# Normalising attention: the reciprocal sums broadcast through DRAM and multiplied on GpSimd, instead of spread by TensorE and multiplied on VectorE

## The chip, the cores and the metric

The kernel runs on one core of one Trainium2 chip. The metric is the device time of one execution in microseconds (us). Three runs of the kernel before gave a median of 2939.29 us, between 2937.05 and 2940.01.

## The reference

Two layers of a diffusion backbone over 1024 latent tokens and 256 context tokens, model width 1024. Layer 0 mixes tokens with a convolution module, layer 1 with grouped-query attention (16 query heads, 4 key/value heads, head size 64, one softmax over all 1280 tokens). A SwiGLU feed-forward network follows each. The change touches only the division by the softmax sums in layer 1 and the start of the product with `wo`:

```python
def gqa_sdpa(q, k, v):
    qg = q.reshape(B, Q, N_KV_HEADS, KV_GROUP, Dh)
    s = jnp.einsum("bqkgd,bskd->bkgqs", qg, k).astype(jnp.float32) * (Dh ** -0.5)
    p = jax.nn.softmax(s, axis=-1).astype(v.dtype)
    o = jnp.einsum("bkgqs,bskd->bqkgd", p, v)
    return o.reshape(B, Q, H * Dh)
...
def attention_module(hx, hc, wq, wk, wv, wo, q_g, k_g, cos, sin, need_ctx):
    ...
    ob = lax.map(lambda q: gqa_sdpa(q, k_all, v_all), qb)
    yx = ob.transpose(1, 0, 2, 3).reshape(B, S, N_HEADS * HEAD_DIM) @ wo
...
def swiglu(h, w1, w3, w2):
    return (jax.nn.silu(h @ w1) * (h @ w3)) @ w2
```

## The kernel before, in words

Every matmul takes a high and a low part of its operands and sums the products of these parts (three in a projection: L172, L173, L174), so TensorE (PE) carries the time. Each engine works through a fixed list of instructions in order. A scheduler writes these lists beforehand from priorities: the main line of the program, background generators that are pumped between its steps (`self.bgq`, `self.pump`), and matmuls that are put back by some steps (`with self.later(self.lav)`).

Attention is cut into 32 units: one of 4 key/value heads `t` by one block of 128 queries, with the 4 query heads that share the key/value head. Two functions make a unit.

- `scores` (L1105): for each of the 4 heads the products of q and k (L1116) into PSUM, a scaling with a row minimum on VectorE (DVE, L1122), and the exponential on ScalarE (ACT, L1124), which also leaves the row sum in `sums`. The probabilities lie with queries on the partitions, 1280 keys along the row.
- `values` (L1128): in 10 steps of 128 keys, four transposes on PE (L1134) into PSUM, the high part by ACT (L1137), the low part by DVE (L1138), and two products with the values (L1140, L1141) into the PSUM bank "av". The result has head dimensions on the partitions and queries along the row, so the 4 sums of a query, which lie on that query's partition, have to get into a row and onto all partitions of their head. Before, this goes: reciprocal on DVE (L1145), a copy by GpSimd (POOL) that repeats each of the 4 numbers 64 times (L1147), two PE transposes of that copy into the bank "av" (L1155) once ACT and DVE have emptied it (L1151, L1152), and a DVE multiply with the transposed numbers (L1156). `done` then stores the tile in the DRAM tile `od` from POOL's queue (L1450); the last unit of a half stays on chip in `olast`.

`attn_stream` (L1160) drives the units: `load_q` (L1102, POOL) fetches q for the next unit, `load_k` (L1095, POOL, two halves) the keys of the next `t`. Units 0 to 15 cover the left half of the queries. The first four run beside the last projections of q, k and v, the others alone, until about 1845 us. `out_proj` then loads `od` (L1485, POOL, four loads), splits it (L161, L164), loads the residual (L1500) and multiplies by `wo`. Units 16 to 31 (right half) run as a background generator beside that product and the left half's feed-forward network, until about 2390 us; there one k buffer ("KB") serves all `t`. Their `out_proj` is followed by the right half's feed-forward network.

Tags as "T1", "T5", "HS" name large SBUF buffers. T1 and T5 hold the probabilities of three heads each during attention.

Of the kernel before, what the change touches and what calls it, by code (L numbers as in the profile page):

```python
# [8 lines left out]
F32 = mybir.dt.float32  # L9
# [3 lines left out]
ALU = mybir.AluOpType  # L13
AX = mybir.AxisListType

P = 128
# [4 lines left out]
TOK = CTX + SEQ  # L21
# [3 lines left out]
NH, NKV, HD = 16, 4, 64  # L25
# [30 lines left out]
class Kern:  # L56
# [1071 lines left out]
    def values(self, t, Ps, sums, dst, done):  # L1128
        nc, c = self.nc, self.c
        av = self.bank("av")  # L1130
        for j in range(NJ):
            tp = self.bank("pt")
            for h in range(4):
                nc.tensor.transpose(tp[:, h * P:(h + 1) * P], Ps[h][:, j * P:(j + 1) * P], c["ident"])  # L1134
            ph, pl = self.ptring[self.ptslot % len(self.ptring)]
            self.ptslot += 1
            nc.scalar.copy(ph, tp)  # L1137
            nc.vector.tensor_tensor(pl, tp, ph.bitcast(F32), op=ALU.subtract)  # L1138
            with self.later(self.lav):
                nc.tensor.matmul(av, lhsT=self.value(t, j), rhs=ph, start=j == 0, stop=False)  # L1140
                nc.tensor.matmul(av, lhsT=self.value(t, j), rhs=pl, start=False, stop=j == NJ - 1)  # L1141
            yield 0.87

        r = sums[:, 1, :]
        nc.vector.reciprocal(r, sums[:, 0, :])  # L1145
        rx = self.sb(256)
        nc.gpsimd.tensor_copy(rx.rearrange("p (h d) -> p h d", d=HD), r.unsqueeze(2).to_broadcast([P, 4, HD]))  # L1147
        tmp = self.sb(256).rearrange("p (a q) -> p a q", q=P)
        v = av.rearrange("p (a b q) -> p a b q", b=2, q=P)
        for b, r, o in ((0, slice(0, 64), slice(64, 128)), (1, slice(64, 128), slice(0, 64))):  # L1150
            nc.scalar.copy(tmp[r], v[o, :, b, :])  # L1151
            nc.vector.tensor_tensor(dst[r], v[r, :, b, :], tmp[r], op=ALU.add)  # L1152
        rb = self.bank("av")
        for a in range(2):
            nc.tensor.transpose(rb[:, a * P:(a + 1) * P], rx[:, a * P:(a + 1) * P], c["ident"])  # L1155
        nc.vector.tensor_tensor(dst, dst, rb[:, 0:256].rearrange("p (a q) -> p a q", q=P), op=ALU.mult)  # L1156
        done()
        yield 0.1

# [270 lines left out]
    def attention(self, final, qr):  # L1430
        nc, a, c = self.nc, self.a, self.c
        kbuf = self.T("T3", [P, 2 * TOK], F32R)
        pr1 = self.T("T1", [P, 3, TOK])
        prh = self.T("HS", [P, 4, TOK])
        ptt = self.T("T2", [P, 4, 2, 512], F32R)
        self.ptring = [(ptt[:, i, 0], ptt[:, i, 1]) for i in range(4)]
# [6 lines left out]
        def dst(q0):  # L1443
            def of(t, q):
                if (t, q % 4) == (NKV - 1, 3):
                    return self.olast, lambda: None
                st = self.sb(256).rearrange("p (a q) -> p a q", q=P)

                def done():
                    nc.gpsimd.dma_start(self.od[:, 2 * t:2 * t + 2, q * P:(q + 1) * P], st)  # L1450
                return st, done
            return of
# [11 lines left out]
        pr4 = None  # L1464
        for us in self.attn_stream(units, (self.kub, kbuf), dst(0), True):
            if self.bgq:
                self.pump(self.rate * us)
            elif pr4 is None:
                pr4 = self.T("T5", [P, 3, TOK])
                self.pring = self.pring[:4] + [pr4[:, 0], pr4[:, 1], pr4[:, 2]] + self.pring[4:]  # L1470
                self.set_banks(**alone)
                self.sring = [0, TOK]
# [8 lines left out]
        def out_proj(q0, otag, tags, ytag, box, xtag):  # L1481
            o = self.T(otag, [P, KT, 512])
            for q in range(4):
                n = 512 if q < 3 else 3 * P
                nc.gpsimd.dma_start(o[:, 2 * q:2 * q + 2, :n], self.od[:, 2 * q:2 * q + 2, q0:q0 + n])  # L1485
            oh = self.T(tags[0], [P, KT, 512], F32R)
            ol = self.T(tags[1], [P, KT, 512], F32R)
            for k in range(KT - 2):
# [14 lines left out]
            for k in range(KT):  # L1503
                o = self.bank("mm")
# [4 lines left out]
                w, p = (self.sm(512) for _ in range(2)) if k else more  # L1509
# [8 lines left out]
        for us in out_proj(0, "HS", ("T6", "T3"), "T4", yL, "HS"):  # L1518
            self.pump(0.4 * us)
# [6 lines left out]
        def tail_R():  # L1526
            self.set_banks(mm=[0, 1, 2, 3], st=[5, 6])
            yield from out_proj(512, "T1", ("T2", "T5"), "T1", yR, "HR")
            yield from self.post_pre2(yR, self.xv[1], self.bank("st"), self.x3d[:, :, 512:], ("T2", "T5"), fR, True)
# [21 lines left out]
        yacc, n = self.acc(CTX), CTX  # L1551
# [172 lines left out]
```

## Time and profile before

| | |
|---|---|
| median of 3 runs | 2939.29 us |
| the profiled execution | 2938.98 us, of which 2937.2 are the span |
| granted TensorE clock over the span | 0.987 |
| PE busy | 2847.7 us (97%) |
| DVE busy | 2160.7 us (74%) |
| ACT busy | 1335.5 us (45%) |
| POOL busy | 222.6 us (8%) |

The span is the time from the first to the last instruction. Busy time is the time of an engine's own instructions, without what it waits; on POOL it holds the issue of transfers where the trace gives that a duration. A share over the whole span hides stages: between 1680 and 1840 us attention runs alone, and between 1980 and 2384 us it lies beside the feed-forward network.

### The profile page before, as it was taken

The numbers are of one execution on the slowest core, as the hardware profiler recorded it, in microseconds if no ns is written. First come the engines' busy times: TensorE is split into PE (matmuls) and PEld (weight loads), VectorE is DVE, ScalarE is ACT, GpSimd is POOL, SyncE is SP. The second block draws the span as 40 slices with busy tenths as digits, with TensorE's granted clock in tenths as the row PEclk, the third lists the DMA queues.
The fourth block names the chain that finished last, engine by engine and source line by source line (L and its number), as shares of the span: only waits on it lengthen the run. The fifth ranks groups of instructions, "written<-read, shape, count | busy, mean of one in ns | idle before, by whom it ended". The sixth has DMA issues, their size and how long they took to land.

```text
span 2937.2 us, 42731 instructions
## 1 busy us (share of the span) xinstructions
PE 2847.7 (97%) x16462; PEld 2446.1 (83%) x16462; DVE 2160.7 (74%) x3746; ACT 1335.5 (45%) x2229; POOL 222.6 (8%) x377
## 2 busy tenths in 40 slices
PE   7999989999999999999999999989999999999998
PEld 6888877888888889989888787767777778889997
DVE  6887788847556378877786899786666666786777
ACT  5222255532222245544445688645555543444444
POOL 0000001011022001000011111110000000010000
PEclk9999999999999999999999999999999999999999
DMA  6443444334356224333345211322222143353332
GB/s 249 140 120 98 116 131 145 135 116 143 115 175 198 65 74 165 114 104 112 109 156 170 88 46 46 97 87 81 66 73 83 60 149 99 110 170 104 102 98 75
DMA packets 131755, 336.58 MB, mean 115 GB/s; under 512 B 31328, under 2 KB 52864, under 8 KB 130656
## 3 DMA queue, kind: packets, MB, share of 16 engines
q1 hardware_dynamic: 78016, 222.33, 24.1%
q0 software_dynamic: 29344, 103.83, 10.7%
q10 hardware_dynamic: 24192, 7.70, 1.1%
q8 instruction: 129, 2.11, 0.3%
q14 instruction: 74, 0.61, 0.1%
HBM read 289.50 MB, written 38.93 MB: 112 GB/s over the span
## 4 chain that ended last, share of the span: by engine, by line
PE 86%; DVE 7%; ACT 2%; issue 2%; DMA 2%; ACTq 0%; POOL 0%; SPq 0%; DVEq 0%; POOLq 0%
PE ps L172 15%; PE ps L173 15%; PE ps L174 15%; PE ps L875 4%; PE ps L877 4%; PE ps L876 4%; PE ps L1116 4%; PE ps L1134 4%; PE ps L1140 2%; PE ps L454 2%; PE ps L455 2%; PE ps L456 2%; PE ps L1141 2%; PE ps L185 1%; PE ps L183 1%
## 5 line engine op out<-in xcount | busy, mean ns | idle before, releaser
L172 PE MATMUL ps<-T,wh 128*128 128x512 f32 (+1 forms) x1360 | 502.5, 370 | 1.4 <-ACT T L161 0.8
L174 PE MATMUL ps<-T,wl 128*128 128x512 f32 (+1 forms) x1360 | 500.4, 368 | 2.0 <-DVE wl L148 2.0
L173 PE MATMUL ps<-T,wh 128*128 128x512 f32 (+1 forms) x1312 | 481.4, 367 | 0.2 <-DVE T L164 0.2
L144 ACT CAST wh<-wr 128x1024 fp32r<-128x1024 f32 (+1 forms) x217 | 225.0, 1037 | 419.9 <-PE ps L173 307.2
L148 DVE TENSOR_TENSOR wl<-wr,wh 128x1024 fp32r<-128x1024 f32 (+1 forms) x217 | 261.9, 1207 | 168.5 <-ACT wh L144 167.1
L875 PE MATMUL ps<-T,wh 128*128 128x256 f32 x1092 | 310.7, 285 | 5.0 <-ACT wh L161 4.5
L876 PE MATMUL ps<-T,wh 128*128 128x256 f32 x1092 | 306.5, 281 | 0.0
L877 PE MATMUL ps<-T,wl 128*128 128x256 f32 x1092 | 305.4, 281 | 0.2 <-DVE wl L164 0.2
L1138 DVE TENSOR_TENSOR T<-ps,T 128x512 fp32r<-128x512 f32 x320 | 216.8, 687 | 107.6 <-ACT T L1137 106.8
L172 PEld LDWEIGHTS ps<-T,wh 128*128 128x128 f32 x1360 | 257.8, 190 | 43.7 <-ACT T L1506 1.7
L174 PEld LDWEIGHTS ps<-T,wl 128*128 128x128 f32 x1360 | 257.7, 190 | 42.4 <-DVE wl L148 2.2
L173 PEld LDWEIGHTS ps<-T,wh 128*128 128x128 f32 x1312 | 248.5, 189 | 38.2 <-DVE T L164 1.3
L1137 ACT CAST T<-ps 128x512 fp32r<-128x512 f32 x320 | 186.0, 586 | 191.1 <-PE ps L1134 177.6
L173 PE MATMUL ps<-HS,wh 128*128 128x512 f32 x656 | 257.9, 393 | 0.0
L172 PE MATMUL ps<-HS,wh 128*128 128x512 f32 x608 | 238.4, 392 | 0.9 <-ACT wh L144 0.9
L174 PE MATMUL ps<-HS,wl 128*128 128x512 f32 x608 | 237.5, 391 | 0.0
L875 PEld LDWEIGHTS ps<-T,wh 128*128 128x128 f32 x1092 | 206.1, 189 | 11.2 <-ACT wh L161 6.7
L876 PEld LDWEIGHTS ps<-T,wh 128*128 128x128 f32 x1092 | 206.6, 189 | 0.5
L877 PEld LDWEIGHTS ps<-T,wl 128*128 128x128 f32 x1092 | 206.2, 189 | 0.6 <-DVE wl L164 0.4
L1134 PE MATMUL ps<-cst,T 128*128 128x128 f32 x1100 | 189.6, 275 | 3.2 <-DVE T L1138 3.1
L1122 DVE TENSOR_SCALAR_CACHE_REDUCE T<-ps,rq 128x1280 f32<-128x1280 f32 x110 | 170.0, 1546 | 27.9 <-PE ps L1116 22.1
L1134 PEld LDWEIGHTS ps<-cst,T 128*128 128x128 f32 x1100 | 132.6, 141 | 49.5 <-DVE T L1138 30.8
(377 smaller groups left out, 6195.9 us busy)
## 6 DMA issues: line engine op xcount, KB each, us to landing
wr<-in_w SPq DMA_DIRECT2D x170, 512.0 KB, 3.6
wr<-in_pw SPq DMA_DIRECT2D x35, 512.0 KB, 3.5
HV<-in_wmodT POOLq DMA_DIRECT2D x56, 256.0 KB, 4.1
q<-in_wmodT POOLq DMA_DIRECT2D x56, 256.0 KB, 3.9
KB<-in_w SPq DMA_DIRECT2D x24, 512.0 KB, 3.6
HR<-in_w SPq DMA_DIRECT2D x23, 512.0 KB, 3.7
q<-in_w SPq DMA_DIRECT2D x23, 512.0 KB, 4.2
q<-qsd POOLq DMA_DIRECT2D x32, 256.0 KB, 3.3
```

Of the source, the lines that this page charges most:

```text
L144: nc.scalar.copy(hi, raw)
L148: nc.vector.tensor_tensor(lo, raw, hi.bitcast(F32), op=ALU.subtract)
L172: nc.tensor.matmul(out[:, :n], lhsT=wh, rhs=xh, start=k == 0, stop=False)
L173: nc.tensor.matmul(out[:, :n], lhsT=wh, rhs=xl, start=False, stop=False)
L174: nc.tensor.matmul(out[:, :n], lhsT=wl, rhs=xh, start=False, stop=k == nk - 1)
L875: nc.tensor.matmul(out, lhsT=wh, rhs=bh, start=first and k == 0, stop=False, **skip)
L876: nc.tensor.matmul(out, lhsT=wh, rhs=bl, start=False, stop=False, **skip)
L877: nc.tensor.matmul(out, lhsT=wl, rhs=bh, start=False, stop=k == 3, **skip)
L1122: nc.vector.tensor_scalar(out=pt, in0=sc, scalar1=rq[:, h:h + 1], scalar2=None, op0=ALU.mult, op1=ALU.min, accum_out=mn)
L1134: nc.tensor.transpose(tp[:, h * P:(h + 1) * P], Ps[h][:, j * P:(j + 1) * P], c["ident"])
L1137: nc.scalar.copy(ph, tp)
L1138: nc.vector.tensor_tensor(pl, tp, ph.bitcast(F32), op=ALU.subtract)
```

## The change

`values` takes the reciprocal at its start and stores the 4 by 128 numbers in a DRAM tile `rsd[unit]` with the head outermost. Two loads bring them back, each number repeated over 64 partitions, into `rb`, at the end of the buffers T1 and T5 (one place while T5 isn't taken, then two in turn). GpSimd multiplies by `rb`. The four loads of `od` for the left half's output projection are issued by SyncE (SP), those of the right half still by POOL.

```diff
--- before.py
+++ after.py
@@ -1128,6 +1128,15 @@
     def values(self, t, Ps, sums, dst, done):
         nc, c = self.nc, self.c
         av = self.bank("av")
+        r = sums[:, 1, :]
+        nc.vector.reciprocal(r, sums[:, 0, :])
+        rd = self.rsd[self.unit]
+        rb = self.rbs[self.unit % len(self.rbs)]
+        self.unit += 1
+        nc.gpsimd.dma_start(rd.rearrange("h q -> q h"), r)
+        rv = rd.rearrange("(a b) q -> b a q", b=2)
+        for b in range(2):
+            nc.gpsimd.dma_start(rb[b * HD:(b + 1) * HD], rv[b:b + 1].to_broadcast([HD, 2, P]))
         for j in range(NJ):
             tp = self.bank("pt")
             for h in range(4):
@@ -1141,19 +1150,12 @@
                 nc.tensor.matmul(av, lhsT=self.value(t, j), rhs=pl, start=False, stop=j == NJ - 1)
             yield 0.87
 
-        r = sums[:, 1, :]
-        nc.vector.reciprocal(r, sums[:, 0, :])
-        rx = self.sb(256)
-        nc.gpsimd.tensor_copy(rx.rearrange("p (h d) -> p h d", d=HD), r.unsqueeze(2).to_broadcast([P, 4, HD]))
         tmp = self.sb(256).rearrange("p (a q) -> p a q", q=P)
         v = av.rearrange("p (a b q) -> p a b q", b=2, q=P)
         for b, r, o in ((0, slice(0, 64), slice(64, 128)), (1, slice(64, 128), slice(0, 64))):
             nc.scalar.copy(tmp[r], v[o, :, b, :])
             nc.vector.tensor_tensor(dst[r], v[r, :, b, :], tmp[r], op=ALU.add)
-        rb = self.bank("av")
-        for a in range(2):
-            nc.tensor.transpose(rb[:, a * P:(a + 1) * P], rx[:, a * P:(a + 1) * P], c["ident"])
-        nc.vector.tensor_tensor(dst, dst, rb[:, 0:256].rearrange("p (a q) -> p a q", q=P), op=ALU.mult)
+        nc.gpsimd.tensor_tensor(dst, dst, rb, op=ALU.mult)
         done()
         yield 0.1
 
@@ -1430,7 +1432,12 @@
     def attention(self, final, qr):
         nc, a, c = self.nc, self.a, self.c
         kbuf = self.T("T3", [P, 2 * TOK], F32R)
-        pr1 = self.T("T1", [P, 3, TOK])
+        def place(tag):
+            t = self.T(tag, [P, 3 * TOK + 2 * P])
+            return t[:, :3 * TOK].rearrange("p (i n) -> p i n", i=3), t[:, 3 * TOK:].rearrange("p (a q) -> p a q", q=P)
+        pr1, rb = place("T1")
+        self.rbs, self.unit = [rb], 0
+        self.rsd = self.dp.tile([2 * NKV * 4, 4, P], F32, tag="rsd", name="rsd")
         prh = self.T("HS", [P, 4, TOK])
         ptt = self.T("T2", [P, 4, 2, 512], F32R)
         self.ptring = [(ptt[:, i, 0], ptt[:, i, 1]) for i in range(4)]
@@ -1466,7 +1473,8 @@
             if self.bgq:
                 self.pump(self.rate * us)
             elif pr4 is None:
-                pr4 = self.T("T5", [P, 3, TOK])
+                pr4, rb = place("T5")
+                self.rbs.append(rb)
                 self.pring = self.pring[:4] + [pr4[:, 0], pr4[:, 1], pr4[:, 2]] + self.pring[4:]
                 self.set_banks(**alone)
                 self.sring = [0, TOK]
@@ -1482,7 +1490,8 @@
             o = self.T(otag, [P, KT, 512])
             for q in range(4):
                 n = 512 if q < 3 else 3 * P
-                nc.gpsimd.dma_start(o[:, 2 * q:2 * q + 2, :n], self.od[:, 2 * q:2 * q + 2, q0:q0 + n])
+                eng = nc.gpsimd if q0 else nc.sync
+                eng.dma_start(o[:, 2 * q:2 * q + 2, :n], self.od[:, 2 * q:2 * q + 2, q0:q0 + n])
             oh = self.T(tags[0], [P, KT, 512], F32R)
             ol = self.T(tags[1], [P, KT, 512], F32R)
             for k in range(KT - 2):
```

POOL's list before, some two units of attention alone. `qsd`, `ksd`, `od` and `rsd` are DRAM tiles, `sb` an output tile of a unit (or, before, the repeated numbers); DMASW are counts of landed transfers.

```order
L1102 DMA q_13572<-qsd_80 128x4x128 [waits DMASW4_49,PE_49]
L1450 DMA od_82<-sb_14960 128x2x128 [waits DVE_49]
L1147 COPY sb_15213<-sums_14964 128x256 [waits DMASW6_49,DVE_49,Pool_49]
L1147 COPY sb_15344<-sums_15095 128x256 [waits DMASW1_49,DVE_49,Pool_49]
L1450 DMA od_82<-sb_15093 128x2x128 [waits DMASW2_49,DVE_49]
L1102 DMA q_13572<-qsd_80 128x4x128 [waits DMASW7_49,DMASW3_49,PE_49]
```

Two copies of the repeated numbers and two loads of q stand next to each other. POOL's list after at the same place, one unit; T1 and T5 are the places of `rb`.

```order
L1136 DMA rsd_13570<-sums_14957 128x4x1 [waits DVE_49]
L1139 DMA T5_14072<-rsd_13570 64x2x128 [waits DMASW4_49,DMASW3_49]
L1139 DMA T5_14072<-rsd_13570 64x2x128 [waits DMASW5_49]
L1102 DMA q_13573<-qsd_80 128x4x128 [waits PE_49]
L1158 TENSOR_TENSOR sb_14953<-sb_14953,T1_13569 128x256 [waits DMASW7_49,DMASW0_49,DVE_49]
L1457 DMA od_82<-sb_14953 128x2x128 [waits Pool_49]
L1136 DMA rsd_13570<-sums_15087 128x4x1 [waits DVE_49]
```

Each unit now has a store to `rsd` that waits for DVE, two loads that wait for its landing, the q load behind them, the multiply of the unit before and its od store.

DVE's list before at the same place: `ps` is PSUM, T2 the split transposes, HS and T1 probabilities, `sums` the 4 sums of a query.

```order
L1152 TENSOR_TENSOR sb_14960<-ps_72,sb_15084 64x256 [waits DMASW0_49,Activation_49,Pool_49]
L1138 TENSOR_TENSOR T2_13571<-ps_72,T2_13571 128x512 [waits DVE_49]
L1122 TENSOR_SCALAR HS_13570,mn_15168<-ps_72,rq2_10629 128x1280 [waits PE_49]
L1152 TENSOR_TENSOR sb_14960<-ps_72,sb_15084 64x256 [waits Activation_49]
L1138 TENSOR_TENSOR T2_13571<-ps_72,T2_13571 128x512 [waits DVE_49,Activation_49]
L1156 TENSOR_TENSOR sb_14960<-sb_14960,ps_72 128x256 [waits DVE_49,PE_49]
L1122 TENSOR_SCALAR T1_13569,mn_15201<-ps_72,rq2_10629 128x1280
L1138 TENSOR_TENSOR T2_13571<-ps_72,T2_13571 128x512 [waits PE_49,Activation_49] x2
L1145 RECIPROCAL sums_14964<-sums_14964 128x4
L1145 RECIPROCAL sums_15095<-sums_15095 128x4 [waits Activation_49]
```

The multiply (L1156) stands in the list, and two units' reciprocals stand next to each other behind the second unit's last scaling. DVE's list after (L1147 is the low part, L1157 the add).

```order
L1122 TENSOR_SCALAR T1_13569,mn_15131<-ps_72,rq2_10629 128x1280 [waits PE_49]
L1157 TENSOR_TENSOR sb_14953<-ps_72,sb_15078 64x256 [waits DMASW5_49,Activation_49,Pool_49]
L1147 TENSOR_TENSOR T2_13572<-ps_72,T2_13572 128x512 [waits DVE_49]
L1147 TENSOR_TENSOR T2_13572<-ps_72,T2_13572 128x512 [waits Activation_49]
L1122 TENSOR_SCALAR HS_13571,mn_15164<-ps_72,rq2_10629 128x1280 [waits PE_49]
L1157 TENSOR_TENSOR sb_14953<-ps_72,sb_15078 64x256 [waits Activation_49]
L1147 TENSOR_TENSOR T2_13572<-ps_72,T2_13572 128x512 [waits Activation_49]
L1122 TENSOR_SCALAR T1_13569,mn_15197<-ps_72,rq2_10629 128x1280 [waits PE_49]
L1147 TENSOR_TENSOR T2_13572<-ps_72,T2_13572 128x512 [waits DVE_49,PE_49,Activation_49]
L1147 TENSOR_TENSOR T2_13572<-ps_72,T2_13572 128x512 [waits PE_49,Activation_49]
L1132 RECIPROCAL sums_15087<-sums_15087 128x4 [waits DMASW0_49,Activation_49]
```

The multiply is gone, and each unit has its own reciprocal (L1132) two steps behind its last scaling.

POOL's list before at the first reload of "KB" in the right half (about 2008 us).

```order
L1147 COPY sb_17026<-sums_16441 128x256 [waits DVE_49,Activation_49]
L1450 DMA od_82<-sb_16439 128x2x128 [waits DMASW3_49,DVE_49]
L1095 DMA KB_12756<-ksd_81 64x2560 [waits DMASW4_49,PE_49]
L1095 DMA KB_12756<-ksd_81 64x2560 [waits DMASW5_49]
L1450 DMA od_82<-sb_16794 128x2x128 [waits DMASW6_49,DVE_49]
L1102 DMA q_13572<-qsd_80 128x4x128 [waits DMASW7_49]
```

The two halves of the k load are issued one behind the other. POOL's list after at this place.

```order
L1158 TENSOR_TENSOR sb_16423<-sb_16423,T5_14072 128x256 [waits DVE_49]
L1457 DMA od_82<-sb_16423 128x2x128 [waits DMASW0_49,Pool_49]
L1095 DMA KB_12756<-ksd_81 64x2560 [waits DMASW1_49,PE_49]
L1158 TENSOR_TENSOR sb_16777<-sb_16777,T1_13569 128x256 [waits DMASW7_49,DMASW6_49,DVE_49]
L1095 DMA KB_12756<-ksd_81 64x2560 [waits DMASW2_49]
L1457 DMA od_82<-sb_16777 128x2x128 [waits DMASW3_49,Pool_49]
L1102 DMA q_13573<-qsd_80 128x4x128 [waits DMASW4_49]
```

The multiply of the unit before (the fourth row) now stands between the two halves of the k load.

## Rows read from the trace of the kernel before

**Rows 1.** Page, part 1: busy us, share of the span, instructions

```profile
PE 2847.7 (97%) x16462; PEld 2446.1 (83%) x16462; DVE 2160.7 (74%) x3746; ACT 1335.5 (45%) x2229; POOL 222.6 (8%) x377
```

**Rows 2.** By stretch: length, busy PE, PEld, DVE, ACT, POOL; clock, DMA share, GB/s

```profile
1680.00:1840.00 160.00, 156.12 (x940) 128.01 (x938) 145.72 (x239) 129.56 (x219) 22.38 (x37) 1.00 0.16 44
1980.00:2384.00 404.00, 403.96 (x2083) 317.76 (x2082) 265.55 (x389) 219.04 (x344) 27.98 (x45) 1.00 0.25 75
```

**Rows 3.** Chain of waits by line, 1980 to 2384 us, then 1680 to 1840

```profile
by line: PE ps L173 17.4%; PE ps L172 17.4%; PE ps L174 17.3%; PE ps L1134 15.5%; PE ps L1116 14.7%; PE ps L1140 8.3%; PE ps L1141 8.1%; PE ps L1155 1.1%; issue 0.1%
...
by line: PE ps L1134 21.3%; PE ps L1116 18.1%; PE ps L1140 15.0%; PE ps L1141 14.0%; DVE T L1138 8.7%; issue 8.2%; ACT T L1137 4.3%; DVE T L1122 4.0%; DVE HS L1122 2.3%; DVE sb L1152 2.2%; PE ps L1155 1.4%; ACT sb L1151 0.6%; ACT T L1124 0.
```

**Rows 4.** By line: count, ns min/median/max, first and last start, shape

```profile
L1155 PE MATMUL ps<-cst,sb x64: 270/273/303, 1646.9 to 2391.7; 128*128 128x128 f32 x64
...
L1147 POOL COPY sb<-sums x32: 394/402/1365, 1605.4 to 2363.0; 128x256 f32<-128x256 f32 x32
...
L1156 DVE TENSOR_TENSOR sb<-sb,ps x30: 409/410/421, 1647.3 to 2364.2; 128x256 f32<-128x256 f32 x30
```

**Rows 5.** Pieces of the chain at two units: start, us, what

```profile
1738.17 0.22 PE ps L1155 x2
...
2045.40 0.41 PE ps L1155 x2
```

**Rows 6.** PE's waits, 1680 to 1840 us: us in total, times, longest

```profile
PE ps L1116 <- DVE HS L1122: 2.8, 5, 0.6
```

**Rows 7.** Timeline: start, us, instruction, idle before and its releaser

```profile
1737.43 0.74 PE L1116 MATMUL ps<-KB,q 128*128 128x256 f32 x3 [0.56 <-DVE HS L1122]
1738.23 0.79 POOL L1102 DMA_DIRECT2D q<-qsd  x1 [9.06 <-PE ps L1116]
...
1742.03 0.18 DVE L1145 RECIPROCAL sums<-sums 128x4 f32<-128x4 f32 x1 [0.39 <-ACT T L1124]
```

**Rows 8.** Timeline, POOL: od stores four units apart

```profile
1709.77 0.71 POOL L1450 DMA_DIRECT2D od<-sb  x1 [0.20 <-issue]
...
1768.60 0.71 POOL L1450 DMA_DIRECT2D od<-sb  x1 [0.19 <-issue]
```

**Rows 9.** DMA issues: issuer, count, KB each, median us to landing

```profile
q<-qsd POOLq DMA_DIRECT2D x32, 256.0 KB, 3.3
...
KB<-ksd POOLq DMA_DIRECT2D x10, 640.0 KB, 7.1
...
od<-sb POOLq DMA_DIRECT2D x30, 128.0 KB, 2.6
...
vc<-HR ACTq DMA_DIRECT2D x7, 128.0 KB, 3.4
```

**Rows 10.** Timeline, the first reload of KB in the right half

```profile
2008.39 1.07 POOL L1095 DMA_DIRECT2D KB<-ksd  x2 [19.04 <-PE ps L1116]
...
2011.60 0.43 DVE L1152 TENSOR_TENSOR sb<-ps,sb 64x256 f32<-64x256 f32 x1 [0.21 <-ACT sb L1151]
...
2018.00 1.41 PE L1116 MATMUL ps<-KB,q 128*128 128x256 f32 x6
```

**Rows 11.** Timeline, the left half's last od store and o load

```profile
1852.66 0.43 DVE L1152 TENSOR_TENSOR sb<-ps,sb 64x256 f32<-64x256 f32 x1
...
1854.44 0.73 POOL L1450 DMA_DIRECT2D od<-sb  x1 [3.59 <-DVE sb L1156]
...
1856.99 0.72 POOL L1485 DMA_DIRECT2D HS<-od  x1 [1.83 <-DMA od<-sb]
...
1860.72 0.83 ACT L161 CAST T<-HS 128x768 fp32r<-128x768 f32 x1 [2.05 <-DMA HS<-od]
...
1862.09 0.50 PE L1140 MATMUL ps<-T,HR 128*128 128x512 f32 x1 [1.18 <-ACT T L1137]
```

**Rows 12.** Timeline, a copy of POOL beside a VectorE operation

```profile
2133.81 1.22 DVE L148 TENSOR_TENSOR wl<-wr,wh 128x1024 fp32r<-128x1024 f32 x1
...
2133.91 1.36 POOL L1147 COPY sb<-sums 128x256 f32<-128x256 f32 x1
```

## The prediction

> **What bounds the kernel now.** I read the page first: PE is busy for 97% of the span [rows 1], so a change pays mainly by what it takes off PE, and costs by what makes PE wait. An average over stages hides where PE does wait, so the busy time by stretch came next [rows 2]. The reader is to see two stages that differ. Between 1980 and 2384 us PE is busy for 403.96 of 404 us: a microsecond of PE work that goes there is a microsecond of time. Between 1680 and 1840 us, with attention alone, PE is busy for 156.1 of 160 us, and DVE stands at 145.7, ACT at 129.6. The 3.9 us without PE work are waits for the other engines, and an operation that leaves DVE could matter there. Third, the chain of waits of both stretches [rows 3]: the two transposes that go (L1155) hold 1.1% of the one and 1.4% of the other. The multiply that leaves DVE (L1156) is in neither list, though other DVE lines hold some 17% of the second (8.7, 4.0, 2.3 and 2.2). POOL is busy for 8%; it is not a matter of its load but of what stands in its list behind a wait.
>
> **What goes from PE.** 64 transposes, two a unit, each 0.27 us by its record [rows 4]. Records overlap, so the price is their share in the chain. In the long stretch that is 1.1% of 404, 4.4 us, for the 14 of the 16 right-half units that end in it: 0.32 us a unit, between the 0.22 and the 0.41 that single pieces show [rows 5]. The two units outside it (about 1921 and 2391 us) stand where PE waits now and then, and I count 0.15 us each. Term one: -4.7 us. Its bounds: -6.6 at 0.41 for all 16, -3.1 at 0.22 for 14.
>
> **Attention alone.** The chain holds 1.4% of 160, 2.2 us, of these transposes there. Yet PE waits 3.9 us in the same stretch, mostly for DVE's scaling [rows 6], and the lists change. The first score products behind a late scaling wait 0.56 us, and a wait of this kind comes in every second unit [rows 6, 7]: units run in pairs now, with two reciprocals next to each other. In the new lists every unit looks alike, each with its own reciprocal two steps behind the last scaling, where the reciprocal waits for the exponential as one of each pair does now (0.39 us [rows 7]). I take the larger wait for all: 10 units at 0.56 are 5.6 us against 3.9 now, +1.7. Against that go the 2.2 us of the transposes. Term two: -0.5 us. Bounds: -6.1 if DVE's relief (a multiply of 0.41 us a unit, [rows 4]) removes all waits as well (2.2 + 3.9), and +1.7 if waits grow to 0.78 us a unit (7.8 - 3.9 - 2.2).
>
> **Units 0 to 3 and the turn to the output projection.** The four units beside the projections lose eight transposes, 0.22 us a unit of chain by the smaller piece [rows 5], 0.9 us; PE also waits there, and I keep half: -0.5. At the turn the last od store of the left half leaves at 1854.44, waiting for DVE's multiply; its landing lets the last load of `od` go at 1856.99, ACT's split waits for that until 1860.72 in front of casts, and PE waits 1.18 us behind these [rows 11]. In the new order POOL multiplies as soon as the second add is done (1852.66 + 0.43 = 1853.09). At 0.4 to 0.6 us the store is ready about 1853.7 instead of 1854.4. SP waits for the landing instead of POOL, with nothing behind it in its list that is due before the load of a later piece of `wo`. I count that half a microsecond comes through: -0.5. Term three: -1.0 us together, bounds -2.1 (0.9 and the whole 1.18) and 0.
>
> **What POOL gets.** A unit adds a store to `rsd`, two broadcast loads and a multiply, and loses the copy of 0.40 us [rows 4]. Nothing of this is in the trace. The multiply is bounded by the copy's own rows: as many elements, but one tile read where the multiply reads two; 0.40 in the median and 1.36 at the worst, which fell beside a DVE operation that reads two tiles [rows 12]. I take 0.5 and keep 1.4. The Trainium skill, "GPSIMD Engine Reference", Engine selection, says that elementwise operations with two inputs belong on VectorE, since GpSimd is about half as fast; by its 4497 ns for 2048 columns a multiply of 256 would take 0.56 us, an estimate. By that the sum stays as it is wherever the multiply has room, and no row of this trace has such an operation on POOL to agree or not.
>
> Where it has room: the od stores of four units are 58.8 us apart (1709.77 to 1768.60 [rows 8]), 14.7 us a unit, and the new work on POOL is two or three issues of 0.7 to 0.8 us and the multiply, so its list isn't full. What counts is the order. The q load, which left at once when the scores freed its place (1738.23 [rows 7]), now stands behind a store that waits for DVE's reciprocal, and behind two loads that wait for the store's landing. Call T the end of the scores. The reciprocal starts at T + 3.8 (1742.03 - 1738.23), and takes 0.18. Then X for the store from issue to landing, 1.1 for the two issues, as for two halves of k (1.07 [rows 10]), and 3.3 for q [rows 9]. q is there at T + 8.4 + X. It is needed about one unit later, at T + 14.7; with half a microsecond to spare, at T + 14.2. So nothing is lost while X is below 5.8 us. The nearest rows: the od store of 128 KB lands in 2.6, a load in 1024 pieces of 128 bytes (`vc`) in 3.4 [rows 9]. The store to `rsd` has 512 elements that lie apart in DRAM. I take 4, which costs nothing; the bounds are 2.6 and, as the longest landing that any of these rows has, 7.1 for the k load, which would cost 1.3 us a unit.
>
> The same shift meets one k load. In the right half "KB" is reloaded three times, and at the first one the multiply of unit 18 now stands between the two halves. That unit's second add ends at 2011.60 + 0.43 = 2012.03 [rows 10]; with 0.4 to 1.4 us for the multiply the second half is issued at 2012.4 to 2013.4 instead of 2009, and lands by the k row's 7.1 us [rows 9] at 2019.5 to 2020.5. The products that need it start at 2018.00 [rows 10]; the same list is 0.4 us longer on PE up to that point, as the order has it by the durations of these rows. PE may do other work of the feed-forward network meanwhile only as far as its fixed list has it ahead. I take 0.4 us: the median landing is of two halves together, so a single half comes sooner. Bounds 0 and 1.9. Term four: +0.4.
>
> DVE loses 32 multiplies of 0.41 us, 13 us, hidden behind PE except in the stage alone, where term two has it. At the very end the split of the right half's `od` waits for POOL's last multiply instead of DVE's: within 1 us either way, counted at nothing.
>
> **Sum.** -4.7 - 0.5 - 1.0 + 0.4 = -5.8 us on the profiled execution's 2938.98, which lies 0.3 us below the median: 2933.2 us.
>
> **Rivals.** (1) *The store to `rsd` lands late* and q arrives behind its products, unit after unit in the stage alone. For it: the store stands in front of q in the list, and scattered single elements have no row here. Against it: 1024 small pieces land in 3.4 us [rows 9]. It decides from X = 5.8. At X = 8 each of 11 units waits 2.2 us, +24.2: 2957 us. The Trainium skill, "DMA: Bandwidth & Descriptors", Rules for kernel authors, speaks for this rival: a last dimension that isn't contiguous becomes one descriptor per element, and its Specifications want 512 bytes a transfer at least. By it the store is 512 descriptors of 4 bytes; how long those take no run here shows yet.
>
> (2) *DVE's relief counts fully.* If the stage alone loses its waits with the multiply, term two is -6.1: 2927.6 us. For it: DVE is at 91% there and its lines hold 17% of the chain. Against it: the multiply itself isn't in that chain.
>
> (3) *Waits eat the gain.* Stage alone +1.7, the k load late by 1.9, nothing at the turn and beside the projections: -4.7 + 1.7 + 1.9 = -1.1, 2937.9 us. For it: PE's waits come from a DVE order that gets no looser. Against it: the long stretch has no wait that could grow, but for that one load.
>
> **How the numbers follow.** Forecast 0.53, rival 1 0.15, rival 2 0.15, rival 3 0.17. What a measurement can tell from no change is 0.2%, 5.9 us, so faster means below 2933.4. The forecast stands on that line: I put 0.28 of it below and 0.25 above, so faster 0.43 with rival 2, same 0.42 with rival 3, slower 0.15. The forecast's own range is 2930 to 2936. The range for 8 in 10 reaches to rival 2 and past rival 3, and to a small part of rival 1 (X about 6.5, +8): 2927 to 2945.
>
> **What would show it.** In the profile after: PE has 64 instructions fewer, and 1980 to 2384 us gets shorter by about 4.5 us with PE still busy throughout (term one). The stage alone keeps PE waits of about half a microsecond for L1122 at each unit (term two). The last load of `od` leaves at least half a microsecond earlier against the split (term three). The store to `rsd` lands in under 5.8 us, and PE has no wait for q. I would be wrong if PE waits for a q load in the stage alone, if POOL's multiply takes over 1.5 us as a rule, or if PE's waits for DVE in that stage vanish.

## The result, and the profile after

Over 21 runs each the changed kernel takes 2944.88 us in the median (2941.54 to 2946.92) and the kernel before 2940.90 (2937.05 to 2944.93). The ratio is 1.0015, with an interval from 1.0009 to 1.0021: 4.4 us slower, between 2.6 and 6.2. The forecast was 5.8 us faster. The profiled execution of the changed kernel has a span of 2943.7 us.

The busy line of the changed kernel's page, and then its two stretches of [rows 2], with the turn to the output projection between them.

```profile
PE 2845.3 (97%) x16398; PEld 2445.9 (83%) x16398; DVE 2150.6 (73%) x3714; ACT 1336.1 (45%) x2229; POOL 293.2 (10%) x469
```

The windows (length, busy time of PE, PEld, DVE, ACT and POOL, clock, DMA share, GB/s):

```profile
1680.00:1840.00 160.00, 153.93 (x915) 125.65 (x915) 141.43 (x229) 130.94 (x217) 48.66 (x70) 1.00 0.25 54
1840.00:1890.00 50.00, 39.84 (x201) 31.08 (x200) 33.84 (x53) 31.69 (x54) 12.06 (x17) 0.90 0.41 105
1980.00:2384.00 404.00, 403.57 (x2065) 319.03 (x2064) 266.01 (x383) 222.43 (x347) 60.59 (x88) 1.00 0.37 81
```

PE has the 64 instructions fewer, and in the long stretch it is still busy for 403.6 of 404 us. The turn is another matter: of 50 us PE works 39.84, and the granted clock, which stands behind the busy times, is 0.90 in the mean. In the kernel before, the same 50 us have 47.15 and 1.00:

```profile
1840.00:1890.00 50.00, 47.15 (x247) 36.92 (x247) 39.11 (x63) 34.30 (x58) 9.12 (x13) 1.00 0.37 119
```

Where the time went is seen best by how much later the same instruction starts in the changed kernel. I took ACT's instructions in both traces, paired by line and count, and the median of nine around each mark, counted from 1590 us on (the parts of the program before that are the same, and single executions differ there by several microseconds either way):

| stretch of the kernel before | later in the changed kernel |
|---|---|
| 1590 to 1842 us, units 0 to 14 | -0.3 us |
| 1842 to 1889 us, the turn | +9.0 us |
| 1889 to 1976 us | +0.7 us |
| 1976 to 2372 us, the right half beside the feed-forward network | -3.4 us |
| 2372 to 2901 us | 0.0 us |

So one place of 50 us lost more than the other stages gained. The stretch from 1889 to 1976 us is 0 to 1.7 us longer in the runs below, 1.7 also where no store to `rsd` exists (the doubled store and the multiply on VectorE apart), and the last one is 1.8 us shorter to 1.0 longer; so nothing is read from these two rows. The timeline of the changed kernel at the turn (start, us, instruction, idle time before and what ended it):

```profile
1846.68 0.77 POOL L1136 DMA_DIRECT2D rsd<-sums  x1 [0.77 <-DVE sums L1132]
...
1848.96 1.44 SPq L1494 DMA_DIRECT2D HS<-od  x3
...
1856.56 1.20 POOL L1139 DMA_DIRECT2D T<-rsd  x2 [9.11 <-DMA rsd<-sums]
1860.32 0.62 ACT L161 CAST T<-HS 128x512 fp32r<-128x512 f32 x1 [8.26 <-DMA HS<-od]
...
1862.33 1.12 PE L1143 MATMUL ps<-cst,T 128*128 128x128 f32 x4 [8.74 <-DVE T L1147]
```

The longest piece of the chain of waits in this stretch (start, us, what):

```profile
1848.96 11.34 DMA HS<-od
```

POOL issues unit 15's store to `rsd` at 1846.68, and its landing, for which the next instruction of POOL waits 9.11 us, comes at 1856.5. In that time SP issues the first three loads of `od` (1848.96). The first of them lands 11.34 us later, ACT's split waits for it (8.26 us idle), ACT's and DVE's work for the rest of unit 15 stands behind that split in their lists, and PE waits 8.74 us. In [rows 11] it was 1.18. What the transfer engines did meanwhile stands in the busy time by stretch (columns as above), here of the changed kernel:

```profile
1850.00:1855.00 5.00, 3.59 (x24) 2.65 (x22) 2.02 (x4) 1.54 (x3) 0.00 (x0) 1.00 0.23 41
...
1863.00:1865.00 2.00, 2.00 (x9) 1.60 (x8) 1.56 (x3) 1.67 (x4) 1.30 (x2) 0.50 0.01 4
```

In the kernel before, where POOL issued the same three loads at 1848.28:

```profile
1850.00:1855.00 5.00, 4.52 (x28) 3.29 (x27) 4.57 (x9) 4.15 (x9) 1.41 (x3) 1.00 0.84 299
```

With the store in flight 41 GB/s were moved behind the issue of the loads, without it 299. The engines' recorded busy share is 0.23 in that time instead of 0.84, so the loads were held up by something that the trace doesn't show as traffic. The row from 1863 us lies behind PE's idle time: PE is busy again throughout, at a granted clock of 0.50, which is 1.2 instead of 2.4 GHz. The transfers (issuer, count, KB each, median us to landing) of the changed kernel:

```profile
od<-sb POOLq DMA_DIRECT2D x30, 128.0 KB, 4.6
...
HS<-od SPq DMA_DIRECT2D x3, 512.0 KB, 12.1
...
rsd<-sums POOLq DMA_DIRECT2D x32, 2.0 KB, 9.8
...
HS<-od SPq DMA_DIRECT2D x1, 384.0 KB, 3.4
```

The three loads in the kernel before:

```profile
HS<-od POOLq DMA_DIRECT2D x3, 512.0 KB, 5.3
```

A transfer of 2 KB takes 9.8 us, more than any of the others here but the loads beside it. The three loads of `od` beside it take 12.1 us instead of 5.3; the fourth, issued by SP too but after the store had landed, 3.4. Also od's stores take 4.6 instead of 2.6 [rows 9]. The theory from this (A): the store to `rsd` keeps the transfer engines for its 9 to 10 us, others queue behind it, and at the turn the loads of `od` are on the path. The rival (B): SP's queue is slow for these loads.

### The profile page after: what moved, and what is told of

Its sections match the earlier page's. It is cut to its first block, busy times and chain, and to the rows that moved or that the text cites. A ratio compares the mean times of both kernels' runs of the same rounds, so it can differ in the third digit from the quotient of the medians.

```text
span 2943.7 us, 42638 instructions
## 1 busy us (share of the span) xinstructions
PE 2845.3 (97%) x16398; PEld 2445.9 (83%) x16398; DVE 2150.6 (73%) x3714; ACT 1336.1 (45%) x2229; POOL 293.2 (10%) x469
## 2 busy tenths in 40 slices
DMA packets 135371, 340.84 MB, mean 116 GB/s; under 512 B 33376, under 2 KB 55152, under 8 KB 134272
## 3 DMA queue, kind: packets, MB, share of 16 engines
q0 software_dynamic: 31872, 106.13, 11.6%
## 4 chain that ended last, share of the span: by engine, by line
PE 85%; DVE 9%; ACT 3%; issue 2%; DMA 1%; ACTq 0%; SPq 0%; DVEq 0%
PE ps L172 15%; PE ps L173 15%; PE ps L174 15%; PE ps L875 4%; PE ps L877 4%; PE ps L876 4%; PE ps L1116 4%; PE ps L1143 4%; PE ps L454 2%; PE ps L456 2%; PE ps L455 2%; PE ps L1149 2%; PE ps L1150 2%; PE ps L185 1%; PE ps L183 1%
## 5 line engine op out<-in xcount | busy, mean ns | idle before, releaser
L1147 DVE TENSOR_TENSOR T<-ps,T 128x512 fp32r<-128x512 f32 x320 | 215.1, 686 | 112.5 <-ACT T L1146 111.6
```

## The experiments

Each was timed in five rounds beside the kernel before on the same chip. Times are medians, ratios are against the kernel before with the 95% interval. Most intervals reach 0.0009 of the time, 2.6 us, to either side; smaller differences between two of these kernels are not told apart.

**SP's issue undone.**

```diff
-                eng = nc.gpsimd if q0 else nc.sync
+                eng = nc.gpsimd
```

> The changed kernel with the four loads of od for the left half issued by POOL again (everything else as changed). Theory A: unit 15's store to rsd, 512 scattered elements, lands only after 9 us and delays every transfer in flight beside it, so the loads of od took 11 to 12 us. Here POOL has them behind unit 15's broadcast loads, so they are issued after that store has landed (about 1858 us instead of 1849), land in 4 to 6 us, and the split starts 1 to 3 us later than in the changed kernel: time 0 to +3 us against the changed kernel (2944.9), so 2945 to 2948. Theory B: SP's queue is slow for this tensor. Then the loads also land in 4 to 6 us here; B and A differ in what stands behind the loads in the second experiment. If the changed kernel's SP issue were the whole loss, the time would fall to about 2936.

2945.31 us, ratio 1.0022 (1.0013 to 1.0030): the loss stays. The timeline of this kernel at the turn:

```profile
1844.52 0.77 POOL L1136 DMA_DIRECT2D rsd<-sums  x1 [1.19 <-DVE sums L1132]
...
1853.43 1.20 POOL L1139 DMA_DIRECT2D T<-rsd  x2 [8.15 <-DMA rsd<-sums]
...
1854.63 2.18 POOL L1494 DMA_DIRECT2D HS<-od  x3
...
1862.85 1.12 PE L1143 MATMUL ps<-cst,T 128*128 128x128 f32 x4 [8.36 <-DVE T L1147]
```

Its transfers of `od`:

```profile
HS<-od POOLq DMA_DIRECT2D x3, 512.0 KB, 6.4
```

POOL comes to the loads only after the store has landed (8.15 us of waiting), they then take 6.4 us, and PE waits 8.36 us. The loads meet the same store either way: by SP as traffic beside them, by POOL as an instruction ahead of them.

**SP's issue alone**, in the kernel before.

```diff
-                nc.gpsimd.dma_start(o[:, 2 * q:2 * q + 2, :n], ...
+                eng = nc.gpsimd if q0 else nc.sync
+                eng.dma_start(o[:, 2 * q:2 * q + 2, :n], ...
```

> The kernel before with only one part of the change: the four loads of od for the left half issued by SP. No store to rsd exists here. Theory A (the store to rsd in flight slows the loads): they land in 4 to 6 us as in the kernel before, time 2940 to 2941.5, -0.5 to +0.5 against before. Theory B (SP's queue is slow for them): they land in 11 to 12 us, PE waits 8 to 9 us at the turn, time 2947 to 2950.

2940.92 us, ratio 1.0002 (0.9993 to 1.0011). The loads land in 4.7 us, by the transfers of this kernel:

```profile
HS<-od SPq DMA_DIRECT2D x3, 512.0 KB, 4.7
```

Theory B falls: without the store SP's loads are no slower than POOL's 5.3 us of the kernel before. They gain nothing either.

**Unit 15 without the store.**

```diff
+        onchip = self.unit == 15
...
-        nc.gpsimd.dma_start(rd.rearrange("h q -> q h"), r)
...
+        if not onchip:
+            nc.gpsimd.dma_start(rd.rearrange("h q -> q h"), r)
...
+        if onchip:
+            rx = self.sb(256)
+            nc.gpsimd.tensor_copy(rx.rearrange("p (h d) -> p h d", d=HD), r4.unsqueeze(2).to_broadcast([P, 4, HD]))
...
+        else:
+            nc.gpsimd.tensor_tensor(dst, dst, rb, op=ALU.mult)
```

> The changed kernel, but unit 15 (the last one before the output projection's first loads) takes the old way: POOL copy, two PE transposes, DVE multiply, no store to rsd and no broadcast loads. Units 0 to 14 and 16 to 31 as changed, SP issues the loads of od. Theory A: no store to rsd is in flight when the loads of od are issued, they land in 4 to 6 us instead of 11 to 12, PE's 8.7 us wait goes back to 1 to 2 us, and the half clock behind it goes too: 8 to 9.5 us less than the changed kernel, 2935.5 to 2937. Theory B (SP's queue): loads still 11 to 12 us, time 2944 to 2945.

2936.69 us, ratio 0.9992 (0.9983 to 1.0001): some 7 us less than the changed kernel by the ratios, 8 by the medians, from one store of 32. The turn in this kernel's busy time by stretch:

```profile
1840.00:1890.00 50.00, 46.66 (x242) 35.97 (x241) 36.42 (x57) 33.51 (x57) 9.36 (x14) 1.00 0.49 124
```

PE's waits there (waited for, us in total, times, longest):

```profile
PE ps L1146 <- DVE T L1150: 1.6, 1, 1.6
```

And the transfers:

```profile
HS<-od SPq DMA_DIRECT2D x3, 512.0 KB, 5.2
...
rsd<-sums POOLq DMA_DIRECT2D x31, 2.0 KB, 10.0
```

The other 31 stores still land in 10.0 us, the loads of `od` in 5.2, PE's longest wait at the turn is 1.6 us, the turn loses 1.1 us instead of 9.0 (counted as above), and the clock is 1.00 there. So the lower clock of the changed kernel (0.90 over these 50 us) came behind the idle PE and went with it.

**What in the store is slow.** First, the same 2 KB in runs of 16 bytes.

```diff
-        nc.gpsimd.dma_start(rd.rearrange("h q -> q h"), r)
+        nc.gpsimd.dma_start(rd.rearrange("h q -> (h q)").rearrange("(q h) -> q h", h=4), r)
```

> The changed kernel with the store to rsd written so that each partition's four numbers lie next to each other in DRAM: 128 runs of 16 bytes instead of 512 scattered elements of 4 bytes, the same 2 KB. The loads read the tile as before, so the numbers go to wrong queries: the output is not normalised as the reference has it, only times are read. Theory A with the scattered elements as its reason: the store lands in 2.5 to 5 us instead of 9.8 and holds up others less; the loads of od land in 4 to 7 us, time 6 to 9.5 us less than the changed kernel, 2935.5 to 2939. Theory C (any small store to DRAM whose landing is waited for lasts 9 us, or the count of elements decides): landing stays at 8 to 10 us, loads of od at 10 to 12, time 2944 to 2946.

2938.14 us, ratio 0.9996 (0.9987 to 1.0004). Transfers of this kernel:

```profile
od<-sb POOLq DMA_DIRECT2D x30, 128.0 KB, 2.3
...
HS<-od SPq DMA_DIRECT2D x3, 512.0 KB, 6.8
...
rsd<-sums POOLq DMA_DIRECT2D x32, 2.0 KB, 1.8
```

PE's waits at the turn:

```profile
PE ps L1143 <- DVE T L1147: 3.1, 1, 3.1
```

The store lands in 1.8 us, and the stores of `od` are back at 2.3. The loads of `od` take 6.8 us. Unit 15's broadcast loads now run beside them (issued at 1846.72, the loads at 1847.02), which may be why; no run separates it. PE's wait is 3.1, and the turn loses 2.7 us.

Second, 512 single elements still, but each 64 bytes from the next.

```diff
-        self.rsd = self.dp.tile([2 * NKV * 4, 4, P], F32, ...
+        self.rsd = self.dp.tile([2 * NKV * 4, 4, P, 16], F32, ...
...
-        nc.gpsimd.dma_start(rd.rearrange("h q -> q h"), r)
+        nc.gpsimd.dma_start(rd[:, :, 0].rearrange("h q -> q h"), r)
```

> The changed kernel with the 512 elements of 4 bytes each in a line of 64 bytes of its own in DRAM (the changed kernel has 16 neighbours from 16 partitions in each line). The broadcast loads read the first 2 KB of that tile, mostly zeros set once at the start of attention, so the output is not the reference's; only times are read. Theory D (the count of single elements decides): the store lands in 8 to 11 us, loads of od in 10 to 13, time 2943 to 2947. Theory E (elements that share a line wait for each other): it lands in 2 to 5 us, loads of od in 5 to 7, time 2937 to 2940.

2936.95 us, ratio 0.9985 (0.9977 to 0.9994). Transfers of this kernel:

```profile
HS<-od SPq DMA_DIRECT2D x3, 512.0 KB, 6.6
...
rsd<-sums POOLq DMA_DIRECT2D x32, 2.0 KB, 2.2
```

PE's waits at the turn:

```profile
PE ps L1143 <- DVE T L1147: 1.6, 1, 1.6
```

As many single elements land in 2.2 us, and the turn loses 0.9 us instead of 9.0 with a store still in it: it was the store's duration that cost. Neither their count nor that they are single makes the store slow by itself, and the trace counts no more packets for the slow layout (33376 of under 512 bytes in the whole changed kernel, as many with runs of 16 bytes, 33392 here). It takes single elements of different partitions that lie side by side in DRAM; the runs of 16 bytes lie side by side too, but are a quarter as many. The experiment moved all elements further apart, so it does not tell the 4 bytes between neighbours from the 512 between the heads. The Trainium skill, "DMA: Bandwidth & Descriptors", Specifications, says that a transfer below 512 bytes becomes a read, a change and a write back. That alone would make both layouts alike; here they differ by a factor of 4.5. That such writes wait for each other where they share a stretch of memory would fit, if few and longer pieces cost little, but no run showed it by itself.

**The store doubled**, its second copy to a tile that nothing reads.

```diff
         nc.gpsimd.dma_start(rd.rearrange("h q -> q h"), r)
+        nc.gpsimd.dma_start(self.rsd2[self.unit - 1].rearrange("h q -> q h"), r)
```

> The changed kernel with one suspected cost doubled: every unit stores its reciprocals a second time, to a tile that nothing reads. Theory A (the store itself keeps the transfer engines, and others queue behind it): the loads of od have two such stores ahead, land in 18 to 21 us instead of 11 to 12, and the time rises by 6 to 10 us to 2951 to 2955. Theory C (the store's landing is only a late message and holds up nobody): the loads land as in the changed kernel, time 2944 to 2946.

3086.93 us, ratio 1.0491 (1.0473 to 1.0509), from four timed runs: 147 us more than before and some 140 more than the changed kernel, where theory A expected 6 to 10. POOL's loads of `rsd` in three units of the timeline:

```profile
1743.21 1.21 POOL L1140 DMA_DIRECT2D T<-rsd  x2 [21.35 <-DMA rsd<-sums]
...
1827.74 0.61 POOL L1140 DMA_DIRECT2D T<-rsd  x1 [23.66 <-DMA rsd<-sums]
...
1904.52 0.61 POOL L1140 DMA_DIRECT2D T<-rsd  x1 [13.13 <-DMA rsd<-sums]
```

PE's waits between 1680 and 1840 us:

```profile
PE ps L1116 <- DMA q<-qsd: 18.7, 6, 8.3
```

The first and the third row are eight units apart: 161.3 us, 20.2 a unit instead of 14.7, about two stores of 10 us one behind the other. POOL waits up to 23.66 us for a landing, and PE waits for q, 18.7 us in this stretch. So two stores did not pass side by side, as they could if only a message came late; theory C falls. Theory A had the direction alone. The loads of `od` land in 9.8 us, where it expected 18 to 21. I had counted the doubled store at the turn alone, and it fills every unit: 71 us are lost before 1842, 23 at the turn and 45 in the long stretch. In the changed kernel the store of a unit takes 9.8 of its 14.7 us, which PE doesn't see; that edge was near.

**Only the right half changed.**

```diff
+        onchip = self.unit < 16
```

> Units 0 to 15 take the old way (POOL copy, two PE transposes, DVE multiply, no store to rsd), units 16 to 31 the new one; the reciprocal is early in both, and SP issues the loads of od. Theory A: the change's gain lies in the long stretch of the right half, where PE is never idle, and its loss at the turn only. The gain of the long stretch stays (-3 to -4.5 us against before), the turn is as in the kernel before: 2935 to 2936.5, a little above or at the kernel with only unit 15 on chip. Rival: the gain comes from attention alone (DVE's relief); then this run is within 1 us of before.

2940.52 us, ratio 0.9998 (0.9989 to 1.0007): 0.6 us below before, where 3 to 4.5 were expected; 3 lies at the interval's edge. In the trace the long stretch has its gain (-3.3 us between 1976 and 2372, counted as above), but 0.8 us are lost before 1842 and 0.9 at the turn: the early reciprocal alone already gives DVE another order, and PE's waits for the scaling, here between 1680 and 1840 us, grow from 3.9 to 5.9 us (3.7 and 2.2):

```profile
PE ps L1116 <- DVE HS L1122: 3.7, 6, 0.7
PE ps L1116 <- DVE T L1122: 2.2, 5, 0.6
```

**Runs of 16 bytes with the right numbers, unit 15 on chip.**

```diff
-        nc.gpsimd.dma_start(rd.rearrange("h q -> q h"), r)
...
+            nc.gpsimd.dma_start(rd.rearrange("(q h) -> q h", h=4), r)
+            rbt = self.sb(512)
+            for b in range(2):
+                nc.gpsimd.dma_start(rbt[b * HD:(b + 1) * HD, 0:511], rd[b:b + 511].unsqueeze(0).to_broadcast([HD, 511]))
+            rb = rbt.rearrange("p (q a c) -> p c a q", a=2, c=2)[:, 0]
```

> A version meant to beat both: unit 15 on chip as before, all other units store their reciprocals in runs of 16 bytes, two loads of 2044 contiguous bytes to 64 partitions each bring all four heads' numbers (into a small tile), and POOL's multiply picks every second pair with a stride. Theory A: the store lands in about 2 us, nothing is held up, the turn is as before, the gain of the long stretch comes in full: 3 to 5 us below before, 2934.5 to 2936.5, the same as or up to 1.5 us below the kernel with only unit 15 on chip. If holding up transfers costs nothing in the long stretch, it equals that kernel.

2939.23 us, ratio 0.9994 (0.9985 to 1.0002). The store lands in 1.8 us, and yet it is not faster than the kernel with scattered stores and unit 15 on chip. Away from the turn the slow stores cost nothing that these runs can tell. In the profiled execution, with a span of 2939.7 us, 4.1 us were lost before 1590 us, where nothing was changed, so it says as little.

**The left half exactly as before, the right half as changed**, with POOL's loads of `od` and the late reciprocal for units 0 to 15.

```diff
+        onchip = self.unit < 16
+        if not onchip:
+            nc.vector.reciprocal(r, sums[:, 0, :])
...
+        if onchip:
+            nc.vector.reciprocal(r4, sums[:, 0, :])
...
-                eng = nc.gpsimd if q0 else nc.sync
+                eng = nc.gpsimd
```

> The left half (units 0 to 15) exactly as in the kernel before, with the late reciprocal, the copy, transposes and DVE multiply, and POOL's loads of od; the right half (units 16 to 31) as changed. Differs from the run with the right half alone changed in that the left half's lists are those of before. Theory A: attention alone and the turn are then as before to within 0.3 us (PE's waits for the scaling between 1605 and 1845 us fall from 11.0 back to about 8.9), and only the long stretch's gain of 3.3 us is left: 2936 to 2937.5 when before is at 2940. Rival: the gain of the long stretch is given back behind it (as its end moves against the loads of the next stage); then within 1 us of before.

2937.63 us, ratio 0.9987 (0.9978 to 0.9996): faster than both kernels, by the ratio 3.8 us below the one before. Its turn in the busy time by stretch:

```profile
1840.00:1890.00 50.00, 47.69 (x249) 37.43 (x249) 38.46 (x61) 34.11 (x58) 11.09 (x16) 1.00 0.48 121
```

PE's waits in attention alone:

```profile
PE ps L1116 <- DVE HS L1122: 2.8, 5, 0.6
PE ps L1116 <- DVE T L1122: 1.0, 5, 0.2
```

And in the long stretch:

```profile
PE ps L1116 <- DMA KB<-ksd: 0.5, 1, 0.5
```

The turn and the waits of attention alone are those of the kernel before, PE waits 0.5 us once for a k load in the long stretch, and that stretch keeps its gain (-3.4 us between 1976 and 2372). Together with the run on the right half alone, which differs in the left half's reciprocal, copy and loads, this puts the 0.8 us lost before 1842 down to the left half's lists.

**The same with runs of 16 bytes in the right half.**

```diff
+            nc.gpsimd.dma_start(rd.rearrange("(q h) -> q h", h=4), r)
+            rbt = self.sb(512)
...
```

> As the run before it, but the right half stores its reciprocals in runs of 16 bytes and reads them back as one row of 2044 bytes a partition. Theory A: nothing of the right half waits for the store, so its landing in 2 instead of 10 us changes nothing on PE: the same time as the run before it to within 1.5 us. Rival: the scattered stores cost the long stretch something by holding up its weight loads; then 1 to 2 us less than the run before it.

2936.83 us, ratio 0.9989 (0.9981 to 0.9998): the same within what these runs tell, and the long stretch gains 3.2 us instead of 3.4. If the slow stores hold up weight loads there, it doesn't reach PE.

**The multiply back on VectorE.**

```diff
-        nc.gpsimd.tensor_tensor(dst, dst, rb, op=ALU.mult)
+        nc.vector.tensor_tensor(dst, dst, rb, op=ALU.mult)
```

> The changed kernel with the multiply on VectorE again (operands as changed, rb in SBUF). Theory A: the multiply's engine is off the path in every stage but attention alone, where 0.41 us a unit go back to a DVE at 88%: 0 to +2 us against the changed kernel, 2944.5 to 2947. Rival (POOL's 0.75 us multiply, slower than DVE's 0.41, delays the od stores and the turn): 1 to 3 us less than the changed kernel.

2951.50 us, ratio 1.0039 (1.0025 to 1.0053), from five timed runs: some 7 us more than the changed kernel, where I expected 0 to 2. In the trace 2.2 us are lost between 1590 and 1842, where the changed kernel gained 0.3. The rest could not be put at a place: the lists of the right half come out in another order, so that the same instruction is 4.6 us later between 1976 and 2372 and 5.5 earlier behind that, -0.9 us together where the changed kernel has -3.4. How much of it is the multiply and how much the other order stays open.

## Why the prediction was wrong

**What bounds it** was right: what PE loses in the long stretch is time.

**Term one (-4.7)** had the right mechanism, at too high a price. The chain share of 1.1% priced a unit at 0.32 us; the stretch with 14 units got 3.4 us shorter. The 0.4 us of term four's wait is in that, so the transposes gave some 3.8, 0.27 a unit, and nearer to the smaller piece of [rows 5], 0.22, than to 0.41. In every run with the right half on `rsd` and the multiply on POOL, the doubled store apart, the stretch got 2.9 to 3.7 shorter; with SP's issue alone it stayed the same (+0.1). Why the share told too much was not looked into.

**Term two (-0.5) and units 0 to 3 (-0.5)** came out at -0.3 together, for -1.0. The wait of the first scores behind a late scaling came at every unit, as the lists had it: PE's waits for DVE's scaling between 1680 and 1840 us rose to 6.6 us, from the 2.8 of [rows 6] and 1.1 for the other buffer; 5.6 were forecast. The row for the other buffer in the kernel before:

```profile
PE ps L1116 <- DVE T L1122: 1.1, 5, 0.2
```

In the changed kernel:

```profile
PE ps L1116 <- DVE HS L1122: 3.6, 6, 0.6
PE ps L1116 <- DVE T L1122: 3.0, 5, 0.6
```

**The turn (-0.5) is the step that failed.** It came out at +9.0 us, where the worst bound of term three was 0. The prediction followed the last load of `od` and its one wait (the od store of unit 14), and did not name the first three loads, so they counted as in the kernel before (issued at 1848.28, landed in 5.3 us). It never asked what else would be in flight at 1849 us: unit 15's store to `rsd`, issued 2.3 us earlier. The store's landing, bounded at 7.1 us, was in the text, but it was weighed against q alone and never laid on one time axis with the loads of the turn. One store less (unit 15 on chip) gives all but 1 us of it back, and so does a store of as many elements that lands in 2.2 us (64 bytes apart).

**The store's landing X** was taken at 4 with an upper bound of 7.1, and is 8.5 to 11.6, 9.8 in the median. The longest landing of other rows was no bound for it, since no row had single elements that lie side by side. The rule of the Trainium skill in rival 1 ("DMA: Bandwidth & Descriptors", Rules for kernel authors) warned of the right instruction. Its reason, one descriptor for each element, is not what decides here: 512 single elements land in 2.2 us when they lie apart.

**Rival 1** had the slow store and the wrong victim. It decided "from X = 5.8", with q late in attention alone; X is 9.8 and PE doesn't wait for q. POOL's list in that stage of the changed kernel:

```profile
1783.84 0.78 POOL L1102 DMA_DIRECT2D q<-qsd  x1 [0.99 <-PE ps L1116]
...
1787.63 0.76 POOL L1136 DMA_DIRECT2D rsd<-sums  x1 [1.03 <-DVE sums L1132]
...
1797.78 1.19 POOL L1139 DMA_DIRECT2D T<-rsd  x2 [8.86 <-DMA rsd<-sums]
...
1798.96 0.79 POOL L1102 DMA_DIRECT2D q<-qsd  x1
```

The q load of 1783.84 waited 0.99 us for PE, that is, for the end of a unit's scores. The next q load, behind the store of 1787.63, leaves at 1798.96, 15.1 us later, and a unit takes 14.7: it may not leave before the next unit's scores have ended in any case. I had put the store in front of the q load that leaves at T, and it stands in front of the one that leaves a unit later. So by the same sum the slack is 14.7 us larger, about 20.5 instead of 5.8. The runs show its two sides only: at 9.8 us PE waits for no q, with the doubled store it does.

**Term four (+0.4)**: the second half of k is issued at 2023.38 behind POOL's multiply, where the first left at 2018.97, and PE's wait in the long stretch is 0.4 us in all. Right in size; in the other runs with the right half changed it is 0 to 0.8, the doubled store and the multiply on VectorE apart. The profile names nothing that ended it here; with the left half as before it names the k load. POOL's list there in the changed kernel:

```profile
2018.97 0.54 POOL L1095 DMA_DIRECT2D KB<-ksd  x1 [15.76 <-PE ps L1116]
...
2022.69 0.73 POOL L1158 TENSOR_TENSOR sb<-sb,T 128x256 f32<-128x256 f32 x1 [3.18 <-DVE sb L1157]
...
2023.38 0.58 POOL L1095 DMA_DIRECT2D KB<-ksd  x1
```

PE's waits between 1980 and 2384 us in the changed kernel:

```profile
PE ps L1116 <- issue: 0.4, 1, 0.4
```

**POOL's multiply** takes 0.75 us, not 0.5, with little spread (count, ns min/median/max, first and last start, shape):

```profile
L1158 POOL TENSOR_TENSOR sb<-sb,T x30: 723/746/757, 1648.3 to 2372.0; 128x256 f32<-128x256 f32 x30
```

That is 1.8 times DVE's 0.41 [rows 4]. What waits for these 30 is the od store. Putting the multiply back on DVE cost some 7 us where I had expected 0 to 2, but the lists changed with it, so what the multiply alone is worth isn't shown.

## What to carry to other kernels

A transfer is not only as long as its bytes: before pricing a small scattered store, ask which elements lie side by side in memory and come from different partitions, and lay its flight on the same time axis as the transfers that the critical path waits for, whoever issues them. A change that repeats 32 times can be right 31 times and lose its gain at the one place where another stage starts; look at the first and last turn of a loop apart from its middle. And when an instruction is put in front of another in a list, check which release that other one was waiting for: it may be one period later than the one next to it in time.

## What the runs showed of the hardware that was not expected

A store of 2 KB as 512 elements of 4 bytes, with neighbours in DRAM from different partitions, lands in 9.8 us; the same bytes as 128 runs of 16 in 1.8; the same 512 elements 64 bytes apart in 2.2. With the slow store in flight other transfers wait too: at the turn 41 GB/s are moved instead of 299, and loads of 512 KB take 12.1 us instead of 4.7 to 5.3. In the whole kernel stores of 128 KB take 4.6 instead of 2.6. With two of them a unit the units take 20.2 us, as if the two did not overlap.
